# An encoder's feed-forward layers: the norm's factor goes through a VectorE copy ahead of the tokens' low parts and is transposed later; the memory's squares come in two halves

## The chip, the cores and the metric

One core of a Trainium2 chip runs the kernel. The metric is the device time of one execution in microseconds (us), the median of several runs. TensorE does the matrix products, VectorE and ScalarE prepare operands and read results, GpSimd does small things and issues DMAs that add into a tile, and SyncE issues the plain loads. Matrix operands lie in SBUF, products in eight PSUM banks (four tagged `pa`, four `pb`).

## The reference

Two encoder layers work on 512 tokens of width 1024 in float32. Each layer is a feed-forward layer, a mixer (attentions of several kinds), an attention to a memory of 256 rows, and a second feed-forward layer, each behind an RMS norm:

```python
def rmsnorm(x, g):
    xf = x.astype(jnp.float32)
    y = xf * lax.rsqrt(jnp.mean(xf * xf, axis=-1, keepdims=True) + EPS)
    return (y * g.astype(jnp.float32)).astype(x.dtype)

def swiglu(x, wg, wu, wd):
    return (jax.nn.silu(x @ wg) * (x @ wu)) @ wd
```

The hidden width of `swiglu` is 2816, which is 22 blocks of 128. The norm's factor of a token (the reciprocal root of the mean of its squares) scales whole rows of the products, so the kernel multiplies the gained but unscaled tokens and applies the factor to the products' results. The memory's rows are normed too, and only the attention to the memory uses them.

## The kernel before, in words

**Products.** A float32 product is made of three passes with rounded operands: high by high, token's low by weight's high, token's high by weight's low. ScalarE makes the high part of an operand (`wh`, `sh`, `t1h` and the like) by a rounding copy, VectorE the low part (`wl`, `sl`, `t1l`) as the rest. Every weight thus costs a load (SyncE), a 128x1024 copy on ScalarE and a 128x1024 subtraction on VectorE.

**A feed-forward layer** (`ffn`; there are four, called first to fourth FFN here). `plain_pair` computes blocks 0 and 1 of the hidden width directly: a gate product and an up product for each (line L316). Behind the second block's gate product TensorE transposes the tokens' summed squares (L249), VectorE sums them (L251, tile `s`) and makes the mean (L258, `v`), GpSimd raises it to the power -0.5 (L242, `r`), TensorE transposes `r` spread over 128 columns (L328, four of them), and VectorE copies the outcome to `R` (L329). `R` scales the gate products (L332, `gs`) and goes into the hidden values.

Blocks 2 to 21 are done as ten pairs by seven products of a quarter's size in place of eight (a Strassen-like scheme). `token_sums` makes the scheme's four combinations of tokens, t1 to t4 (L366), with their high (L370, ScalarE) and low parts (L373 and L375, VectorE). For each pair `open_pair` multiplies quarter w11 with tokens x11; `sum_pair` makes the sum of two quarters (`s`, loaded by SyncE and added into by a GpSimd DMA, L460), multiplies it with t1 (here: product T1), subtracts w11 from it (L464) and multiplies with t2 (product T2); `cross_pair` multiplies w12 with x21 (here: the x product), fetches `s3`, negates it on ScalarE (L482), adds to it by a GpSimd DMA (L483) and multiplies with t3 (T3); `close_pair` does the rest. Each of these is 24 matmuls of 128x256 (L430). `operand` (L408, L409) makes a weight's parts; its numbers in the first pair are used below: n0 is w11, n1 the sum, n2 the sum less w11, n3 w12, n4 `s3`, n5 the next pair's w11. Every third (n2, n5) has its own buffers `sh` and `sl`; the others take turns in two buffers `wh` and two `wl`.

**Order.** TensorE's order is the program's. The other engines' order is made by a scheduler that follows when results are due; `high_priority()` moves work ahead, and `behind(ins)` keeps what follows on an instruction's engine behind it.

**The memory's squares.** `mem_stats` runs once, in the first FFN after pair 2: eight blocks of 128x256 are loaded by SyncE (L1104), squared on ScalarE (L218, L221), summed on GpSimd (L222), then transposed and reduced as above. TensorE meets the two transposes of the sum between two products of pairs.

Of the kernel before, what the change touches and what calls it, by code (L numbers as in the profile page):

```python
# [11 lines left out]
F32 = mybir.dt.float32  # L12
# [7 lines left out]
P = 128  # L20
# [3 lines left out]
KB = D // P  # L24
FB = F // P
QB = S // P
NMEM = 256
# [38 lines left out]
LEAD, REST = ((0, 0), (0, 1)), ((1, 0),)  # L66

CHUNKS = (8, 8, 6)
LAMBDA_INIT = 0.8 - 0.6 * math.exp(0.0)

L0_CHUNKS = [[(2120, 256), (2632, 256)], [(3144, 512)], [(2376, 256), (2888, 256)],
# [33 lines left out]
class Encoder:  # L105
# [157 lines left out]
    def ffn(self, pre):  # L263


        with ExitStack() as ctx:
            pool = lambda name: ctx.enter_context(self.tc.tile_pool(name=pre + name, bufs=1))
            f = self.f = SimpleNamespace(pre=pre, hp=pool("h"), tp=pool("t"), H={}, n=0, last=None)
            self.plain_pair()
            ends = [sum(CHUNKS[:c + 1]) // 2 for c in range(len(CHUNKS))]  # L270
            c = 0
            pair = self.open_pair(1)
            for p in range(1, FB // 2):
                final = p == FB // 2 - 1
                self.sum_pair(pair)
                if p in ends:
                    self.down(c)
                    c += 1
                self.cross_pair(pair)
                if final:  # L280
                    early = self.block(c, 0, True)
                    self.down_products(c, early, LEAD + REST, False)
                    self.close_pair(pair, True)
                    self.down(c, early)
                else:
                    old, pair = pair, self.open_pair(p + 1)
                    self.close_pair(old, False)
                if p == 2 and self.mem_r is None:
                    self.mem_stats()

    def plain_pair(self):
        nc, I, f = self.nc, self.I, self.f
        xs, order = self.xs, self.order
        self.wshare = 0
        banks = []
        for b in range(2):
            ws, self.ws = self.ws, None
            after = self.rest if b == 0 and self.chained else None
            ws = ws or [self.wload(I[f.pre + w][b], 1024, after) for w in ("wg", "wu")]
            pp = [self.bank("pa"), self.bank("pb" if b else "pa")]  # L300
            banks.append(pp)
            if b == 0:
                head = order[:KB // 2]
                groups = [(ks, ((0, 0), (0, 1))) for ks in (head, order[KB // 2:KB - 1], order[KB - 1:])]
                if self.mem_r is None:
                    groups[1:1] = [(head, ((1, 0),))]
                    groups.append((order[KB // 2:], ((1, 0),)))
                else:
                    groups.append((order, ((1, 0),)))
            else:  # L310
                groups = [(order, ((0, 0), (0, 1), (1, 0)))]
            for ks, ops in groups:
                for w, p in zip(ws, pp):
                    for a, c in ops:
                        for k in ks:
                            nc.tensor.matmul(p, w[a][:, k * P:(k + 1) * P], xs[k][c],  # L316
                                             start=k == order[0] and a == c == 0, stop=k == order[-1] and a == 1)
                    if b == 1 and p is pp[0]:
                        with self.tc.high_priority():
                            v, r = self.stats(self.acc, QB)  # L320
        f.after, f.led = self.loaded, self.leading
        with self.behind(self.summed), self.behind(self.squared):
            self.token_sums()
        p = self.bank("pb")
        f.R = f.tp.tile([P, S], F32, name="R", tag="R", bufs=1)
        with self.tc.high_priority():
            for i in range(QB):
                nc.tensor.transpose(p[:, i * P:(i + 1) * P], r[:, i:i + 1].to_broadcast([P, P]), self.ident)  # L328
            nc.vector.tensor_copy(f.R, p)  # L329
        gs = f.tp.tile([P, 1024], F32, name="gs", tag="gs")  # L330
        for b in range(2):
            nc.vector.tensor_mul(gs[:, b * S:(b + 1) * S], banks[b][0], f.R)  # L332
        self.hidden(0, gs, [pp[1] for pp in banks])
# [12 lines left out]
    def hidden_parts(self, p, h, b0):  # L346
        nc, f = self.nc, self.f
        if p not in f.H:
            f.H[p] = [f.hp.tile([P, 1024], F32R, name=n, tag="H", bufs=CHUNKS[0]) for n in ("hh", "hl")]
        hh, hl = f.H[p]  # L350
# [5 lines left out]
    def token_sums(self):  # L356

        nc, f = self.nc, self.f
        xs, gain = self.xs, self.col(self.norm)
        half = KB // 2  # L360
        one, two = slice(0, 256), slice(256, 512)
        part = lambda t, k: t[:, (k % half) * 256:(k % half) * 256 + 256]
        g = lambda k: gain[:, k:k + 1]

        def combine(out, k, tokens, op, other):
            nc.vector.scalar_tensor_tensor(part(out, k), self.x[k][:, tokens], g(k), part(other, k), op0=OP.mult, op1=op)  # L366

        def parts(name, t, sign=1.0):
            h = f.tp.tile([P, 1024], F32R, name=name + "h", tag=name + "h")
            nc.scalar.activation(h, t, AF.Copy, scale=sign)  # L370
            l = f.tp.tile([P, 1024], F32R, name=name + "l", tag=name + "l")
            if sign == 1.0:
                nc.vector.tensor_sub(l, t, h.bitcast(F32))  # L373
            else:
                nc.vector.scalar_tensor_tensor(l, t, sign, h.bitcast(F32), op0=OP.mult, op1=OP.subtract)  # L375
            return [(part(h, k), part(l, k)) for k in range(half)]

        lead, rest = range(half), range(half, KB)
        room = [f.tp.tile([P, 2048], F32, name="tq", tag="gu", bufs=2) for _ in range(2)]
        x12, t1, t2, t3 = (t[:, o:o + 1024] for t in room for o in (0, 1024))  # L380
        for k in lead:
            nc.scalar.activation(part(x12, k), self.x[k][:, two], AF.Copy, scale=g(k))
        for k in lead:
            combine(t1, k, one, OP.subtract, x12)
        T1 = parts("t1", t1, -1.0)
        for k in rest:
            combine(t2, k, two, OP.add, t1)
        T2 = parts("t2", t2)
        for k in rest:
            combine(t3, k, two, OP.subtract, x12)  # L390
        T3 = parts("t3", t3)
        t4 = x12
        for k in rest:
            combine(t4, k, one, OP.subtract, t2)
        T4 = parts("t4", t4)
        quarters = lambda ks, tokens: [tuple(x[:, tokens] for x in xs[k]) for k in ks]
        f.B = {"11": quarters(lead, one), "21": quarters(rest, one), "22": quarters(rest, two),
               "1": T1, "2": T2, "3": T3, "4": T4}
# [141 lines left out]
    def block(self, c, d, own=False):  # L540

        nc, f = self.nc, self.f
        n = CHUNKS[c] * P
        src = self.I[f.pre + "wd"][d, :, sum(CHUNKS[:c]) * P:sum(CHUNKS[:c]) * P + n]
        if not own:
# [7 lines left out]
    def down_products(self, c, block, ops, tail):  # L553

        f = self.f
        (w, bank), nb = block, CHUNKS[c]
        for a, e in ops:
            for j in range(nb - 2, nb) if tail else range(nb - 2):
                b = sum(CHUNKS[:c]) + j
                h = f.H[b // 2][e][:, b % 2 * S:b % 2 * S + S]  # L560
# [532 lines left out]
            nc.vector.scalar_tensor_tensor(kl[:, sl], p, gcol, kh.bitcast(F32)[:, sl], op0=OP.mult, op1=OP.subtract)  # L1093
        return kh, kl, vp

    def mem_stats(self):
        nc = self.nc
        with ExitStack() as ctx:
            mp = ctx.enter_context(self.tc.tile_pool(name="ms", bufs=2))
            acc, loaded, leading, powed = None, self.loaded, self.leading, self.powed  # L1100
            for k in range(KB):
                m = mp.tile([P, NMEM], F32, name="mem", tag="mem", bufs=4)
                with self.behind(loaded):
                    nc.sync.dma_start(m, self.I["memT"][k * P:(k + 1) * P, :])  # L1104
                with self.behind(powed), self.behind(leading):
                    acc = self.square(acc, m, NMEM, mp)
            v, r = self.stats(acc, 2)
            self.mem_r = self.const.tile([P, 2], F32, name="mem_r")
            nc.vector.tensor_copy(self.mem_r, r[:, 0:2])
            self.mem_epsv = self.const.tile([P, 2], F32, name="mem_epsv")  # L1110
            nc.vector.tensor_scalar(self.mem_epsv, v[:, 0:2], EPS, None, op0=OP.mult)
# [417 lines left out]
```

## Time and profile before

| what | value |
|---|---|
| runs, us | 2157.35, 2159.32, 2159.65 |
| median, us | 2159.32 |
| the profiled execution's own time, us | 2162.13 |
| its span from first to last instruction, us | 2160.3 |
| TensorE busy | 2101.7 us, 97% of the span |
| VectorE, ScalarE, GpSimd busy | 73%, 53%, 17% |
| mean granted TensorE clock | 0.992 of full |

The span is what the profile shows, and 1.8 us lie around it. Busy shares are means over many stages. The chain that ended last tells which engine sets the time where; a wait of TensorE on that chain is time that something else costs. A timeline row gives start, duration, engine, line, operation and tiles, and in brackets the idle time before it with what ended it.

### The profile page before, as it was taken

What the parts mean: (1) busy time and instruction counts of PE and PEld (TensorE: products, weight loads), DVE (VectorE), ACT (ScalarE), POOL (GpSimd) and SP (SyncE); (2) the same over time, 40 slices, a digit from 0 to 9 for tenths busy, and PEclk for the clock granted to TensorE, in tenths of its full rate; (3) what the DMA queues carried; (4) which work ended last, traced back from release to release, by engine and by line L of the source; (5) the groups of instructions that cost most, each with busy time, mean ns of one, the idle gap of its engine ahead of it and who ended that gap; (6) DMA issues with size and microseconds to landing.
All of it is one profiled execution on the core that took longest, in us unless ns stands there. A gap on an engine that the chain in (4) does not pass through costs nothing.

```text
span 2160.3 us, 32514 instructions
## 1 busy us (share of the span) xinstructions
PE 2101.7 (97%) x12830; PEld 1877.6 (87%) x12834; DVE 1575.2 (73%) x2242; ACT 1137.2 (53%) x1701; POOL 376.2 (17%) x319
## 2 busy tenths in 40 slices
PE   7999999998999989999999999999999998999999
PEld 5989998787778879898989899988888877989997
DVE  7757668479876788585788677685668677857666
ACT  5535444465686565253455355344678555625442
POOL 1200002336332120000020000013443022000000
PEclk9999999999999999999999999999999999999999
DMA  6646633321232257365346466334223225646532
GB/s 204 181 123 180 163 99 125 141 74 65 70 130 73 79 151 187 111 187 146 91 143 183 139 167 173 103 110 161 79 87 128 88 69 146 165 123 180 162 102 91
DMA packets 86122, 279.65 MB, mean 129 GB/s; under 512 B 9681, under 2 KB 12881, under 8 KB 85969
## 3 DMA queue, kind: packets, MB, share of 16 engines
q1 hardware_dynamic: 74448, 235.62, 32.5%
q0 software_dynamic: 11520, 41.95, 11.0%
q8 instruction: 101, 1.65, 0.3%
q14 instruction: 53, 0.43, 0.1%
HBM read 271.24 MB, written 6.29 MB: 128 GB/s over the span
## 4 chain that ended last, share of the span: by engine, by line
PE 86%; DVE 8%; ACT 2%; issue 1%; POOL 1%; DMA 1%; SPq 0%; DVEq 0%; POOLq 0%; ACTq 0%
PE ps_pa L430 26%; PE ps_pb L430 11%; PE ps_pa L663 10%; PE ps_pa L561 10%; PE ps_pb L561 9%; PE ps_pa L614 4%; PE ps_pa L316 2%; PE ps_pb L769 2%; PE ps_pa L1203 1%; PE ps_pb L821 1%; PE ps_pa L1060 1%; PE ps_pb L794 1%; DVE wl L157 1%; DVE xl L205 1%; PE ps_pa L979 1%
## 5 line engine op out<-in xcount | busy, mean ns | idle before, releaser
L155 ACT ACTIVATE wh<-wf 128x1024 fp32r<-128x1024 f32 (+2 forms) x211 | 215.5, 1023 | 356.4 <-PE ps_pa L561 120.9
L157 DVE TENSOR_TENSOR wl<-wf,wh 128x1024 fp32r<-128x1024 f32 (+2 forms) x169 | 200.3, 1188 | 50.4 <-ACT wh L155 47.8
L409 DVE TENSOR_TENSOR wl<-s,wh 128x1024 fp32r<-128x1024 f32 x108 | 132.3, 1225 | 71.9 <-ACT wh L408 69.5
L408 ACT ACTIVATE wh<-s 128x1024 fp32r<-128x1024 f32 x108 | 114.3, 1059 | 103.8 <-PE ps_pb L430 40.5
L408 ACT ACTIVATE wh<-wf 128x1024 fp32r<-128x1024 f32 x84 | 89.1, 1061 | 132.0 <-PE ps_pa L430 45.8
L483 POOL DMA_DIRECT2D s<-l_ffn_wq x40 | 35.6, 889 | 532.0 <-ACT s L482 532.0
L157 POOL TENSOR_TENSOR wl<-wf,wh 128x1024 fp32r<-128x1024 f32 x42 | 101.8, 2425 | 141.6 <-ACT wh L155 140.0
L663 PE MATMUL ps_pa<-wh,xh 128*128 128x512 f32 x384 | 123.4, 403 | 0.0
L663 PE MATMUL ps_pa<-wh,xl 128*128 128x512 f32 x384 | 119.9, 393 | 0.0
L663 PE MATMUL ps_pa<-wl,xh 128*128 128x512 f32 x384 | 119.4, 392 | 0.0
L460 POOL DMA_DIRECT2D s<-l_ffn_wq x40 | 35.7, 891 | 463.7 <-DMA s<-l_ffn_wq 391.6
L409 DVE TENSOR_TENSOR wl<-wf,wh 128x1024 fp32r<-128x1024 f32 x84 | 102.8, 1224 | 12.9 <-ACT wh L408 12.8
L571 DVE TENSOR_TENSOR dn<-ps_pa,R 128x512 f32<-128x512 f32 x48 | 33.1, 690 | 88.6 <-PE ps_pa L561 88.3
L222 POOL TENSOR_TENSOR acc<-acc,sq 128x512 f32<-128x512 f32 (+1 forms) x37 | 52.2, 1411 | 251.9 <-ACT sq L221 250.8
L561 PE MATMUL ps_pb<-hh,wh 128*128 128x512 f32 x352 | 95.5, 389 | 0.0
L561 PE MATMUL ps_pb<-hl,wh 128*128 128x512 f32 x352 | 95.4, 389 | 0.0
L561 PE MATMUL ps_pb<-hh,wl 128*128 128x512 f32 x352 | 95.4, 389 | 0.0
L561 PE MATMUL ps_pa<-hh,wh 128*128 128x512 f32 x328 | 88.8, 390 | 0.0
L561 PE MATMUL ps_pa<-hh,wl 128*128 128x512 f32 x328 | 88.6, 389 | 0.0
L561 PE MATMUL ps_pa<-hl,wh 128*128 128x512 f32 x328 | 88.6, 389 | 0.0
L663 PEld LDWEIGHTS ps_pa<-wh,xl 128*128 128x128 f32 x384 | 72.7, 189 | 16.1
L663 PEld LDWEIGHTS ps_pa<-wl,xh 128*128 128x128 f32 x384 | 72.6, 189 | 16.0
(376 smaller groups left out, 5973.1 us busy)
## 6 DMA issues: line engine op xcount, KB each, us to landing
wf<-l_ffn_wq SPq DMA_DIRECT2D x120, 512.0 KB, 3.3
s<-l_ffn_wq SPq DMA_DIRECT2D x80, 512.0 KB, 4.5
s<-l_ffn_wq POOLq DMA_DIRECT2D x80, 512.0 KB, 6.6
wf<-l_ffn_wd SPq DMA_DIRECT2D x64, 512.0 KB, 4.0
wf<-l_w_in SPq DMA_DIRECT2D x48, 512.0 KB, 3.2
wf<-l_ffn_wd SPq DMA_DIRECT2D x32, 384.0 KB, 3.1
wf<-l_mem_wkv SPq DMA_DIRECT2D x16, 512.0 KB, 3.3
wf<-l_w_out SPq DMA_DIRECT2D x16, 512.0 KB, 3.2
```

Of the source, the lines that this page charges most:

```text
L155: self.leading = nc.scalar.activation(wh[:, sl], w[:, sl], AF.Copy)
L157: eng.tensor_sub(wl[:, sl], w[:, sl], wh.bitcast(F32)[:, sl])
L222: self.summed = (eng or nc.gpsimd).tensor_add(acc[:, :n], acc[:, :n], sq[:, :n])
L316: nc.tensor.matmul(p, w[a][:, k * P:(k + 1) * P], xs[k][c], start=k == order[0] and a == c == 0, stop=k == order[-1] and a == 1)
L408: self.leading = nc.scalar.activation(h, t, AF.Copy)
L409: nc.vector.tensor_sub(l, t, h.bitcast(F32))
L430: self.nc.tensor.matmul(bank[:, sl], w[a][:, o:o + P], xs[k][b], start=first and z == a == b == k == 0, stop=z == a == 1 and k == KB // 2 - 1,
L460: nc.gpsimd.dma_start(pair.s, self.quarter(p, 2), accum_op=OP.add)
L561: self.nc.tensor.matmul(bank, w[a][:, j * P:(j + 1) * P], h, start=j == a == e == 0, stop=j == nb - 1 and (a, e) == ops[-1])
L614: nc.tensor.matmul(banks[dd], a[:, o:o + P], parts(k)[b], start=k == first and a is wh and b == 0, stop=k == last and a is wl)
L663: nc.tensor.matmul(banks[i], xs[k][a][:, i * P:(i + 1) * P], w[b][:, kk * 512:kk * 512 + 512], start=k == a == b == 0, stop=k == KB - 1 an ...
L769: nc.tensor.matmul(bank[:, o:o + n], a, b[:, :n], start=c == 0, stop=c == len(ops) - 1)
```

## The change

It has three parts. First, `r` is copied by VectorE into a tile `factor` as soon as it is there, and everything that `parts` issues (the high and low parts of t1 to t4) is kept behind that copy on the copy's engine: VectorE. Second, the four transposes, the copy to `R` and the hidden values of the plain pair move into a function that is called after `open_pair(1)`, so that they stand behind the first pair's first product. Third, the memory's squares are issued in two halves of four blocks, after pairs 3 and 4, and their sum is transposed after pair 6; the condition that they stand behind a power on GpSimd is dropped.

```diff
-            self.plain_pair()
+            R = self.plain_pair()
...
             pair = self.open_pair(1)
+            R()
...
-                if p == 2 and self.mem_r is None:
-                    self.mem_stats()
+                if self.mem_r is None:
+                    self.mem_stats(p)
...
                         with self.tc.high_priority():
-                            v, r = self.stats(self.acc, QB)
+                            r = self.stats(self.acc, QB)[1]
+                            factor = self.small.tile([P, 4], F32, name="factor", tag="factor")
+                            f.factored = nc.vector.tensor_copy(factor, r)
         f.after, f.led = self.loaded, self.leading
         with self.behind(self.summed), self.behind(self.squared):
             self.token_sums()
+        return lambda: self.plain_end(banks, factor)
+
+    def plain_end(self, banks, r):
+        nc, f = self.nc, self.f
         p = self.bank("pb")
...
         def parts(name, t, sign=1.0):
+            with self.behind(f.factored):
+                return parts_of(name, t, sign)
...
+MEM_SQUARES, MEM_FACTOR = (3, 4), 6
...
+            for k in range(MEM_SQUARES.index(p) * n, MEM_SQUARES.index(p) * n + n):
...
-                with self.behind(powed), self.behind(leading):
-                    acc = self.square(acc, m, NMEM, mp)
-            v, r = self.stats(acc, 2)
+                with self.behind(leading):
+                    f.macc = self.square(f.macc, m, NMEM, f.mp)
+        if p == MEM_FACTOR:
+            v, r = self.stats(f.macc, 2)
```

What it moves on the engines follows in rows of the two programs' orders. Line numbers of the changed kernel are higher by 2 to 13.

VectorE in the first FFN, before, from the low part of t1 on. `wl<-s_396` is operand n1, `s_396<-s_396,wf` the subtraction of w11, `wl<-wf` operand n3.

```order
L375 SCALAR_TENSOR_TENSOR t1l<-tq,t1h 128x1024
L366 SCALAR_TENSOR_TENSOR tq<-x,cols,tq 128x256
L373 TENSOR_TENSOR t3l<-tq,t3h 128x1024
L258 TENSOR_SCALAR v<-s 128x4
L366 SCALAR_TENSOR_TENSOR tq<-x,cols,tq 128x256
L409 TENSOR_TENSOR wl<-s_396,wh 128x1024
L373 TENSOR_TENSOR t2l<-tq,t2h 128x1024
L373 TENSOR_TENSOR t4l<-tq,t4h 128x1024
L464 TENSOR_TENSOR s_396<-s_396,wf 128x1024
L329 COPY R<-ps_pb 128x512
L409 TENSOR_TENSOR wl<-wf,wh 128x1024
L332 TENSOR_TENSOR gs<-ps_pa,R 128x512 x2
```

The same place in the changed kernel:

```order
L260 TENSOR_SCALAR v<-s 128x4
L375 SCALAR_TENSOR_TENSOR tq<-x,cols,tq 128x256
L422 TENSOR_TENSOR wl<-s_398,wh 128x1024
L325 COPY factor<-r 128x4
L388 SCALAR_TENSOR_TENSOR t1l<-tq,t1h 128x1024
L386 TENSOR_TENSOR t2l<-tq,t2h 128x1024
L386 TENSOR_TENSOR t3l<-tq,t3h 128x1024
L386 TENSOR_TENSOR t4l<-tq,t4h 128x1024
L477 TENSOR_TENSOR s_398<-s_398,wf 128x1024
L338 COPY R<-ps_pb 128x512
L422 TENSOR_TENSOR wl<-wf,wh 128x1024
L422 TENSOR_TENSOR wl<-s_491,wh 128x1024
```

`v` is two large instructions earlier; the copy of the factor stands behind n1, and all four low parts behind the copy. Behind these rows `gs` and then the low part of n2 follow in the changed kernel, so n4 (`wl<-s_491`) now precedes both. In the second and fourth FFN `v` also moves ahead of t1l and t3l, n0 stands ahead of the copy, and n1 behind t4l.

VectorE in the third FFN, before:

```order
L375 SCALAR_TENSOR_TENSOR t1l<-tq,t1h 128x1024
L373 TENSOR_TENSOR t3l<-tq,t3h 128x1024
L373 TENSOR_TENSOR t2l<-tq,t2h 128x1024
L373 TENSOR_TENSOR t4l<-tq,t4h 128x1024
L409 TENSOR_TENSOR wl<-wf,wh 128x1024
L251 TENSOR_REDUCE s<-ps_pb 128x4
L258 TENSOR_SCALAR v<-s 128x4
L409 TENSOR_TENSOR wl<-s_11058,wh 128x1024
L329 COPY R<-ps_pb 128x512
L464 TENSOR_TENSOR s_11058<-s_11058,wf 128x1024
L332 TENSOR_TENSOR gs<-ps_pa,R 128x512 x2
L409 TENSOR_TENSOR wl<-wf,wh 128x1024
```

and in the changed kernel:

```order
L422 TENSOR_TENSOR wl<-wf,wh 128x1024
L253 TENSOR_REDUCE s<-ps_pb 128x4
L260 TENSOR_SCALAR v<-s 128x4
L325 COPY factor<-r 128x4
L388 SCALAR_TENSOR_TENSOR t1l<-tq,t1h 128x1024
L386 TENSOR_TENSOR t2l<-tq,t2h 128x1024
L386 TENSOR_TENSOR t3l<-tq,t3h 128x1024
L386 TENSOR_TENSOR t4l<-tq,t4h 128x1024
L422 TENSOR_TENSOR wl<-s_11064,wh 128x1024
L338 COPY R<-ps_pb 128x512
L422 TENSOR_TENSOR wl<-wf,wh 128x1024
L477 TENSOR_TENSOR s_11064<-s_11064,wf 128x1024
```

Here the four low parts, which stood ahead of everything, moved behind the power and its copy. `gs`, n4 and the low part of n2 follow.

ScalarE in the first FFN, before, around operands n2 (`sh<-s_396`) and n4 (`wh<-s_489`):

```order
L450 COPY gu<-ps_pa 128x2x256
L408 ACTIVATE sh<-s_396 128x1024
L408 ACTIVATE wh<-s_489 128x1024
L340 ACTIVATE t<-gs 128x1024
L408 ACTIVATE sh<-wf 128x1024
L467 COPY gu<-ps_pa 128x2x256
L482 ACTIVATE s_1009<-s_1009 128x1024
```

and in the changed kernel, where `s_955` is pair 3's `s3`:

```order
L463 COPY gu<-ps_pa 128x2x256
L421 ACTIVATE wh<-s_491 128x1024
L421 ACTIVATE sh<-s_398 128x1024
L349 ACTIVATE t<-gs 128x1024
L495 ACTIVATE s_955<-s_955 128x1024
L421 ACTIVATE sh<-wf 128x1024
L480 COPY gu<-ps_pa 128x2x256
```

n4 now stands ahead of n2, and the negation of `s3` ahead of n5 (`sh<-wf`) and of the copy of T2's outcome; so it is in all four FFNs.

## Rows read from the trace of the kernel before

**Rows 1.** The page: the chain that ended last, by engine.

```profile
PE 86%; DVE 8%; ACT 2%; issue 1%; POOL 1%; DMA 1%; SPq 0%; DVEq 0%; POOLq 0%; ACTq 0%
```

**Rows 2.** Waits of TensorE: total us, times, longest.

```profile
PE ps_pb L328 <- POOL r L242: 18.4, 3, 7.5
```

**Rows 3.** Timeline, first FFN, TensorE: start, us, engine, line, operation.

```profile
31.93 1.98 PE L316 MATMUL ps_pb<-xh,wl 128*128 128x512 f32 x8
...
46.49 0.64 PE L430 MATMUL ps_pb<-t1h,wh 128*128 128x256 f32 x4
...
49.37 0.64 PE L430 MATMUL ps_pa<-t2h,sh 128*128 128x256 f32 x4
...
52.98 0.64 PE L430 MATMUL ps_pa<-xh,wh 128*128 128x256 f32 x4
```

**Rows 4.** Timeline, first FFN, VectorE, with GpSimd's power.

```profile
35.59 5.75 POOL L242 TENSOR_TENSOR r<-v,mhalf 128x4 f32<-128x4 f32 x1 [4.81 <-DVE v L258]
...
38.08 1.22 DVE L373 TENSOR_TENSOR t4l<-tq,t4h 128x1024 fp32r<-128x1024 f32 x1
39.21 1.23 DVE L464 TENSOR_TENSOR s<-s,wf 128x1024 f32<-128x1024 f32 x1
...
48.50 1.28 DVE L332 TENSOR_TENSOR gs<-ps_pa,R 128x512 f32<-128x512 f32 x2
```

**Rows 5.** Timeline, first FFN, ScalarE.

```profile
49.09 1.06 ACT L408 ACTIVATE wh<-s 128x1024 fp32r<-128x1024 f32 x1 [0.33 <-PE ps_pb L430]
```

**Rows 6.** Timeline, second FFN: ScalarE, GpSimd, TensorE.

```profile
783.00 1.04 ACT L408 ACTIVATE wh<-wf 128x1024 fp32r<-128x1024 f32 x1
...
785.94 5.35 POOL L242 TENSOR_TENSOR r<-v,mhalf 128x4 f32<-128x4 f32 x1 [3.58 <-DVE v L258]
...
803.33 0.64 PE L430 MATMUL ps_pa<-xh,wh 128*128 128x256 f32 x4
```

**Rows 7.** Timeline, third FFN: ScalarE, GpSimd, TensorE.

```profile
1132.82 1.06 ACT L408 ACTIVATE wh<-wf 128x1024 fp32r<-128x1024 f32 x1 [0.38 <-DMA wf<-l_ffn_wq]
...
1137.90 1.04 POOL L242 TENSOR_TENSOR r<-v,mhalf 128x4 f32<-128x4 f32 x1 [6.21 <-DVE v L258]
...
1143.25 0.64 PE L430 MATMUL ps_pb<-t1h,wh 128*128 128x256 f32 x4
...
1149.01 0.64 PE L430 MATMUL ps_pa<-xh,wh 128*128 128x256 f32 x4
```

**Rows 8.** Timeline, fourth FFN: GpSimd, TensorE.

```profile
1825.21 5.35 POOL L242 TENSOR_TENSOR r<-v,mhalf 128x4 f32<-128x4 f32 x1 [4.19 <-DVE v L258]
...
1841.90 0.64 PE L430 MATMUL ps_pa<-xh,wh 128*128 128x256 f32 x4
```

**Rows 9.** Timeline, the memory's squares: ScalarE, then TensorE.

```profile
86.68 0.75 ACT L221 ACTIVATE sq<-mem 128x256 f32<-128x256 f32 x2 [3.29 <-DMA mem<-memT]
...
91.30 0.69 PE L249 MATMUL ps_pb<-ident,acc 128*128 128x128 f32 x2 [3.60 <-POOL acc L222]
91.64 1.20 PE L430 MATMUL ps_pb<-t1h,wh 128*128 128x256 f32 x4
...
96.74 0.64 PE L430 MATMUL ps_pa<-t2h,wh 128*128 128x256 f32 x4
```

**Rows 10.** Windows: stretch, us, busy (count) of PE, PEld, DVE, ACT, POOL, clock, DMA, GB/s.

```profile
91.00:95.00 4.00, 3.70 (x18) 3.70 (x19) 3.99 (x5) 0.00 (x0) 0.24 (x1) 0.50 0.92 157
571.00:575.00 4.00, 4.00 (x15) 3.37 (x14) 3.38 (x7) 3.04 (x5) 0.00 (x0) 0.58 0.00 0
```

**Rows 11.** Timeline, TensorE, in the first mixer.

```profile
569.14 0.63 PE L794 MATMUL ps_pb<-ident,e 128*128 128x128 f32 x2 [2.90 <-DVE e L921]
```

**Rows 12.** Timeline, first FFN, SyncE's queue, then ScalarE.

```profile
52.08 0.33 SPq L417 DMA_DIRECT2D s<-l_ffn_wq  x1
...
55.40 1.06 ACT L482 ACTIVATE s<-s 128x1024 f32<-128x1024 f32 x1 [1.17 <-DMA s<-l_ffn_wq]
```

**Rows 13.** The page: DMA issues, KB each, median us to landing.

```profile
s<-l_ffn_wq SPq DMA_DIRECT2D x80, 512.0 KB, 4.5
```

More of the change, by code (lines that the diff above doesn't have):

```diff
@@ L267, in ffn @@
             pool = lambda name: ctx.enter_context(self.tc.tile_pool(name=pre + name, bufs=1))
-            f = self.f = SimpleNamespace(pre=pre, hp=pool("h"), tp=pool("t"), H={}, n=0, last=None)
-            self.plain_pair()
+            f = self.f = SimpleNamespace(pre=pre, ctx=ctx, hp=pool("h"), tp=pool("t"), H={}, n=0, last=None)
+            R = self.plain_pair()
             ends = [sum(CHUNKS[:c + 1]) // 2 for c in range(len(CHUNKS))]
@@ L368, in parts, with parts_of @@
         def parts(name, t, sign=1.0):
+            with self.behind(f.factored):
+                return parts_of(name, t, sign)
+        def parts_of(name, t, sign):
             h = f.tp.tile([P, 1024], F32R, name=name + "h", tag=name + "h")
@@ L1094, in mem_keys, with mem_stats @@
         return kh, kl, vp
[L1096 to L1102, printed above, removed]
+    def mem_stats(self, p):
+        nc, f = self.nc, self.f
+        if p in MEM_SQUARES:
+            if p == MEM_SQUARES[0]:
+                f.mp = f.ctx.enter_context(self.tc.tile_pool(name="ms", bufs=2))
+                f.macc = None
+            loaded, leading = self.loaded, self.leading
+            n = KB // len(MEM_SQUARES)
+            for k in range(MEM_SQUARES.index(p) * n, MEM_SQUARES.index(p) * n + n):
+                m = f.mp.tile([P, NMEM], F32, name="mem", tag="mem", bufs=4)
                 with self.behind(loaded):
                     nc.sync.dma_start(m, self.I["memT"][k * P:(k + 1) * P, :])
-                with self.behind(powed), self.behind(leading):
-                    acc = self.square(acc, m, NMEM, mp)
-            v, r = self.stats(acc, 2)
+                with self.behind(leading):
+                    f.macc = self.square(f.macc, m, NMEM, f.mp)
+        if p == MEM_FACTOR:
+            v, r = self.stats(f.macc, 2)
             self.mem_r = self.const.tile([P, 2], F32, name="mem_r")
```

## The prediction

> **What bounds the kernel now.** I read the chain that ended last first: TensorE holds 86% of it, VectorE 8%, GpSimd 1% [rows 1]. So only what TensorE waits for, or does more slowly, can move the time. Of TensorE's waits the largest is that of the four transposes for the norm's factor: 18.4 us in three waits, 7.5 the longest [rows 2]. The reader is to see that three of the four FFNs have it. In the first FFN the up product ends at 33.91 (31.93+1.98), the first pair's T1 starts at 46.49, T2 at 49.37 and the x product at 52.98 [rows 3]. A T product undisturbed takes 2.88 (49.37-46.49), a sixth of it 0.48.
>
> Why the power is late stands in [rows 4]: it starts at 35.59 and lasts 5.75, while VectorE runs one 128x1024 instruction after another, every 1.13 (39.21-38.08), the last ending at 40.44. The power ends 0.90 behind that. In the second and fourth FFN it takes 5.35 [rows 6, 8], in the third, where VectorE has no work, 1.04 [rows 7]. I read this as: beside back-to-back VectorE work the power gets through only when VectorE pauses.
>
> The Trainium skill (SBUF — State Buffer, section "SBUF: two separate sides") says that VectorE and GpSimd share a port pair as an exclusive lock, and that whichever instruction starts first has it for its whole length. The rows agree that the two exclude each other, but not that the power gets its turn at the end of the running instruction. From 35.59 to 40.44 it sat through some four of them. By the rule alone it would get in sooner, which is a rival below.
>
> The other wait is the memory's: 3.60 ahead of the two transposes, and behind it T1 took 5.10 (91.64 to 96.74) where 2.88 is usual [rows 9], at a granted clock of 0.50 [rows 10], which is the lower level, 1.2 GHz.
>
> **The FFNs, worked out.** I follow VectorE to the x product's start, after which TensorE was fully fed before. Durations: 1.13 for each 128x1024 on VectorE in a row, 1.22 for the last one to its end; 1.19 for the two `gs` [rows 4]; 0.65 for the copy of `R`, half of that pair; 1.06 for a rounding on ScalarE [rows 5]. The factor's copy is in no row; it lies between nothing and 1.13, and with 4 columns in place of 1024 I take 0.1.
>
> First FFN. `v` loses t1l and t3l ahead of it, so the power starts 2.26 sooner, at 33.33. n1's low part needs a buffer that the up product frees at 33.91; it runs to 35.17. VectorE then has only the factor's copy, so the power ends 0.90 later, 36.07. Low parts start at 36.2: four of them and the subtraction end at 41.94, n2's rounding at 43.0. T2 would be due at 39.97 (33.91, two products of 2.88 and 0.3 for four transposes, from 0.69 for two at the lower clock [rows 9]). So a new wait of 3.1 opens there. Behind the subtraction come R, n3, n4, `gs`, and n2's low part, which ends at 47.17. T2's third sixth needs it, having come there at 44.0: another 3.1. The x product starts 4x0.48 later, 49.1, against 52.98: gain **3.9**.
>
> Second FFN. The power starts at 783.68. n0's rounding ends at 784.04 [rows 6], its low part at 785.30, the power at 786.2. Four low parts follow from 786.35, n1's low part runs 790.87 to 792.1, and T1's third sixth waits for it; T2 is due at 794.05. Then R, n3, the subtraction to 795.0, the rounding to 796.1: T2 waits 2.0. `gs`, n4, n2's low part end at 798.46, T2's third sixth waits 1.4; x starts at 800.4, against 803.33: gain **2.9**. The fourth is the same, 1039.27 later by the two powers' starts: 1839.7 against 1841.90, gain **2.2** [rows 6, 8].
>
> Third FFN. Before, all low parts were done ahead of the power and nothing waited. Now n0's rounding ends at 1133.88 [rows 7], its low part at 1135.1, the sum and `v` at 1135.9, the power at 1137.0. Low parts to 1141.6, n1's to 1142.85, in time for T1 at 1143.25 as before. But R, n3 and the subtraction take VectorE to 1146.45, and n2's rounding, behind n4's on ScalarE, ends at 1147.9: T2, due at 1146.13, waits 1.8. `gs`, n4 and n2's low part end at 1149.95 (1.1 more); x starts at 1151.9 against 1149.01: **loss 2.9**.
>
> Sum: 3.9+2.9+2.2-2.9 = 6.1 gained, if TensorE's clock stays up.
>
> **What the new waits cost in clock.** A wait of 2.90 [rows 11] was followed by a stretch at 0.58, one of 3.60 by T1 at 0.50, which cost 2.22 [rows 9, 10]. The new waits are between 1.1 and 3.1. Each FFN's pair of them may cost nothing or 2.2. I take 1.5 in the first, which is nearest to the rows, 1.0 in the second and fourth, 0.5 in the third: **4.0**.
>
> **ScalarE's new order.** The negation of pair 3's `s3` now stands ahead of n5's rounding and the copy of T2's outcome, without which T3 can't start. Its load is issued when n4's low part ends; it landed 3.3 after its issue (52.08 to 55.40) [rows 12]. In the second FFN that gives 797.3+3.3+1.06+0.97+0.5 = 803.2 (the copy taken as half a rounding, having half the columns), and T3 is due at 800.4+2.88 = 803.3: 0.1 to spare, likewise in the third and fourth. In the first 1.3 are left. The median landing is 4.5 [rows 13], which would cost 1.1 in each of three. Bounds: nothing to 3.3; I take the middle, **1.5**, since the rows of this place lie at the lower end and the page's median above it.
>
> **The memory.** Before, squares waited 3.29 for the second load group [rows 9]. Now each half fits the four buffers, so its loads wait for no square of its own half, the halves stand a pair apart, and the transposes come some three pairs later. A pair is seven products of 2.88, 20 us, so the sum is long done. Gain: 3.60+2.22 = **5.8**. The number of GpSimd's additions and ScalarE's squares stays; each half lies beside TensorE's products, in a stage where GpSimd is nearly free. Were that cover gone, one half's additions would delay a pair's accumulating DMA (rival below).
>
> **Sum.** 6.1-4.0-1.5+5.8 = 6.4 us gained. The profiled execution took 2162.13 and would take 2155.7; it lies 2.8 above the median of the runs, 2159.32, from which I forecast **2152.9**. A measurement of this kernel can tell about 0.2%, 4.3 us, from no change.
>
> **Rivals.**
> (a) The clock stays full through waits of 1 to 3 us. For it: no row shows a fall behind a wait below 2.9. Then 4.0 come back: 2148.9. Chance 0.12.
> (b) The power gets in at the end of the VectorE instruction that runs when it is issued. In the first FFN it would run ahead of n1's low part, which saves 0.3 to 0.4; in the second and fourth 0.3 each: 1.0 more gain, 2151.9. Against it: the three long powers. Chance 0.06. This is what the Trainium skill's lock (SBUF — State Buffer, "SBUF: two separate sides") would make of it; the rows agree only as far as that the two block each other.
> (c) The clock falls by the full 2.2 in all four FFNs, 8.8 in place of 4.0: 2157.7, no change that counts. For it: the waits come in pairs, 3 to 6 us in sum. Chance 0.12.
> (d) The memory's sum, or the accumulating DMA behind the additions, still holds up a product: the 5.8 are not gained, 2158.7. For it: loads of memory stand in SyncE's queue between weights. Chance 0.08.
> (e) The change does not do what it says: the power's length isn't VectorE's doing and stays 5.35 to 5.75. Then everything in the first FFN is 3.0 later than worked out, in the second and fourth 2.8, and the FFNs lose 2.5 instead of gaining 6.1: 2161.5, no change. Against it: the third FFN's 1.04. Chance 0.06.
> (f) Slower: the negation's load. Each us of landing over 3.4 (4.6 in the first FFN) delays T3 in each FFN, because n5 and the copy queue behind. At 7.0 the loss is 3x3.6+2.4 = 13.2 in place of 1.5: 2164.6. It decides from 6.8 on. For it: the median of this load is already 4.5 [rows 13]. Against it: 3.3 at this place [rows 12]. Chance 0.10.
>
> **The numbers.** The forecast has 0.46. Faster: forecast, (a), (b), 0.64. Within 0.2% (2155.0 to 2163.6): (c), (d), (e), 0.26. Slower: 0.10. The range 2148.0 to 2159.0 holds all but (e), (f) and a little of the forecast's own spread.
>
> **What would show it.** Right: powers of about 1.0 to 2.7 us in all FFNs; the wait for the factor gone from TensorE's list; new waits of T1 and T2 for `sh`, `wl`, `sl` of 1 to 3 us, those of the third FFN among them; x products at about 49.1 in the first FFN; no wait at the memory's transposes, now behind pair 6. Wrong: powers still above 5; granted clock of 1.0 or of 0.5 throughout the first pair; ScalarE idle at the negation, with TensorE waiting at T3; a product of pairs 4 to 6 waiting for an accumulated sum.

## The result, and the profile after

| | before | changed |
|---|---|---|
| median, us | 2159.08 | 2141.99 |
| runs, us | 2157.35 to 2159.65 | 2138.36 to 2143.13 |
| the profiled execution's time, us | 2162.13 | 2142.44 |
| its span, us | 2160.3 | 2140.7 |

The ratio of changed to before is 0.9919, with a 95% interval of 0.9902 to 0.9936: 17.5 us less by this ratio, where 6.4 were forecast and the range began at 2148.0. The direction was right, the size was not. One execution of e2 and one of e4 below took 2535 and 2957 us at mean granted clocks of 0.765 and 0.654; medians and ratios leave them out.

The page of the changed kernel, its first and its chain section (busy us, share, instructions by engine; then the chain by engine):

```profile
PE 2089.6 (98%) x12834; PEld 1859.6 (87%) x12834; DVE 1573.6 (74%) x2246; ACT 1137.5 (53%) x1701; POOL 366.1 (17%) x319
...
PE 86%; DVE 9%; ACT 2%; issue 1%; DMA 1%; POOL 0%; SPq 0%; DVEq 0%; POOLq 0%; ACTq 0%
```

GpSimd is gone from the chain [rows 1]. But TensorE's busy time itself fell, from 2101.7 to 2089.6, although it has the same work: 12.1 us that no wait explains. That is the number to follow.

The waits of TensorE in the changed kernel (total us, times, longest):

```profile
PE ps_pa L443 <- ACT sh L421: 8.3, 4, 3.1
...
PE ps_pa L443 <- DVE sl L422: 6.0, 4, 2.8
PE ps_pb L443 <- DVE wl L422: 3.2, 2, 1.8
```

The 18.4 us for the factor [rows 2] and the memory's 3.6 are gone; in their place stand 17.5 us: for operand n2 (`sh`, `sl`) in all four FFNs, for n1 (`wl`) in two. These are the new waits of the forecast.

The timeline of the first FFN, changed kernel: GpSimd, VectorE, TensorE, ScalarE.

```profile
33.88 1.21 POOL L244 TENSOR_TENSOR r<-v,mhalf 128x4 f32<-128x4 f32 x1 [2.40 <-DVE v L260]
...
33.70 0.48 DVE L375 SCALAR_TENSOR_TENSOR tq<-x,cols,tq 128x256 f32<-128x256 f32 x1
34.15 1.23 DVE L422 TENSOR_TENSOR wl<-s,wh 128x1024 fp32r<-128x1024 f32 x1
35.29 0.17 DVE L325 COPY factor<-r 128x4 f32<-128x4 f32 x1
...
30.71 1.98 PE L319 MATMUL ps_pb<-xh,wl 128*128 128x512 f32 x8
...
42.26 0.74 PE L443 MATMUL ps_pa<-t2h,sh 128*128 128x256 f32 x4 [3.09 <-ACT sh L421]
...
46.37 1.23 PE L443 MATMUL ps_pa<-t2h,sl 128*128 128x256 f32 x4 [2.84 <-DVE sl L422]
...
49.95 0.71 PE L443 MATMUL ps_pa<-xh,wh 128*128 128x256 f32 x4
...
33.07 1.04 ACT L421 ACTIVATE wh<-s 128x1024 fp32r<-128x1024 f32 x1
...
50.30 0.57 ACT L480 COPY gu<-ps_pa 128x512 f32<-128x512 f32 x1
```

The power takes 1.21 where it took 5.75 [rows 4], and T2 waits 3.09 and 2.84. From the up product's last pass to the x product it is 19.24 us (30.71 to 49.95); before it was 21.05 [rows 3]. Behind the second wait the last four sixths of T2 took 3.58 us in place of 1.92. The windows view shows the granted clock around it, 0.57, not far above the lower of its two levels, 1.2 GHz (stretch, us, busy and count of PE, PEld, DVE, ACT, POOL, granted clock, DMA share, GB/s):

```profile
43.00:51.00 8.00, 5.16 (x30) 4.90 (x29) 7.43 (x9) 3.77 (x5) 0.92 (x1) 0.57 0.44 147
```

The same distance in the other FFNs, changed against before: 17.46 against 19.41, 13.81 against 10.88, 17.37 against 18.70. The gains are 1.8, 1.9, -2.9 and 1.3, in sum 2.2 us. In the first two FFNs the slow stretch reaches into the x product: T3 starts 2.94 and 3.28 behind its start, where 2.88 is usual, so that counted up to T3 the gain is 1.7. The third FFN, which had no wait, now has two:

```profile
1131.70 0.74 PE L443 MATMUL ps_pa<-t2h,sh 128*128 128x256 f32 x4 [1.62 <-ACT sh L421]
1133.77 0.74 PE L443 MATMUL ps_pa<-t2h,sl 128*128 128x256 f32 x4 [0.85 <-DVE sl L422]
```

The memory's squares, changed kernel, GpSimd's two groups of additions and TensorE's transposes:

```profile
97.32 3.85 POOL L224 TENSOR_TENSOR acc<-acc,sq 128x256 f32<-128x256 f32 x3 [1.43 <-ACT sq L223]
161.34 5.59 POOL L224 TENSOR_TENSOR acc<-acc,sq 128x256 f32<-128x256 f32 x4 [0.24 <-ACT sq L223]
...
207.31 0.38 PE L251 MATMUL ps_pb<-ident,acc 128*128 128x128 f32 x2
```

The sum is there 40 us before it is wanted, and the transposes wait for nothing [rows 9].

So 2.2 us from the FFNs and some 6 from the memory are seen. The rest is in the matmuls themselves. Grouped by line and tiles (count, then busy us and mean ns of one, the pipelined time included), before:

```profile
L561 PE MATMUL ps_pb<-hh,wh 128*128 128x512 f32 x352 | 95.5, 389 | 0.0
...
L430 PE MATMUL ps_pa<-xl,sh 128*128 128x256 f32 x192 | 30.9, 283 | 0.0
L430 PE MATMUL ps_pa<-t2l,wh 128*128 128x256 f32 x192 | 30.9, 283 | 0.0
...
L430 PE MATMUL ps_pa<-t3l,sh 128*128 128x256 f32 x96 | 15.4, 283 | 0.0
```

and changed:

```profile
L574 PE MATMUL ps_pb<-hh,wh 128*128 128x512 f32 x352 | 96.3, 392 | 0.0
...
L443 PE MATMUL ps_pa<-xl,sh 128*128 128x256 f32 x192 | 30.0, 278 | 0.0
...
L443 PE MATMUL ps_pa<-t2l,wh 128*128 128x256 f32 x192 | 29.6, 276 | 0.0
...
L443 PE MATMUL ps_pa<-t3l,sh 128*128 128x256 f32 x96 | 15.4, 282 | 0.0
```

Every 128x256 product of t with `wh`, and of x with `sh`, is 3 to 10 ns shorter; t with `sh` is not, and the 128x512 products of the hidden values are 3 ns longer. From start to start (worked out from the trace's starts within groups of equal tiles), before's matmuls stand 120 ns apart almost without exception; the changed kernel's t with `wh` stand mostly 113, 114, 117 or 118 ns apart. The built program shows what differs: the tile `factor` has two buffers of 32 bytes among the small tiles, and everything allocated behind them (`hh`, `hl`, t1 to t4, `sh`, `sl`, `gu`) lies 64 bytes higher in each partition. Taken modulo 256 bytes, x, `xh`, `wh`, `wl` and t1 to t4, `sh`, `hh` all lay at 0; now x and `wh` lie at 0, t, `sh` and `hh` at 64.

**Theory P**: a 128x256 matmul goes faster where its two operands lie at different offsets, so the new tile, not the new order, brought some 10 us. **Rival S**: the order did it.

### The profile page after: what moved, and what is told of

Its sections match the earlier page's. It is cut to its first block, busy times and chain, and to the rows that moved or that the text cites. A ratio compares the mean times of both kernels' runs of the same rounds, so it can differ in the third digit from the quotient of the medians.

```text
span 2140.7 us, 32519 instructions
## 1 busy us (share of the span) xinstructions
PE 2089.6 (98%) x12834; PEld 1859.6 (87%) x12834; DVE 1573.6 (74%) x2246; ACT 1137.5 (53%) x1701; POOL 366.1 (17%) x319
## 4 chain that ended last, share of the span: by engine, by line
PE 86%; DVE 9%; ACT 2%; issue 1%; DMA 1%; POOL 0%; SPq 0%; DVEq 0%; POOLq 0%; ACTq 0%
PE ps_pa L443 26%; PE ps_pa L676 11%; PE ps_pb L443 10%; PE ps_pa L574 10%; PE ps_pb L574 10%; PE ps_pa L627 4%; PE ps_pa L319 2%; PE ps_pb L782 2%; PE ps_pb L834 1%; DVE xl L207 1%; PE ps_pa L1073 1%; PE ps_pb L807 1%; DVE wl L159 1%; PE ps_pa L1221 1%; PE ps_pa L992 1%
## 5 line engine op out<-in xcount | busy, mean ns | idle before, releaser
L584 DVE TENSOR_TENSOR dn<-ps_pb,R 128x512 f32<-128x512 f32 x48 | 33.0, 688 | 73.5 <-PE ps_pb L574 73.1
```

The source lines that it names most:

```text
L584: nc.vector.tensor_mul(t, bank, f.R)
```

## The experiments

**e1, addresses alone.** The kernel before, with 64 bytes more padding; order and instructions equal.

```diff
-PAD_SMALL = 80
+PAD_SMALL = 96
```

> The kernel before with a padding tile that is 64 bytes longer, so that every tile allocated behind the small tiles (t1 to t4, sh, sl, hh, hl) lies 64 bytes higher, as it does in the changed kernel; no instruction and no order differs from before. Theory P (the new factor tile moved the operands, and TensorE's 128x256 matmuls go at 113 to 118 ns instead of 120 wherever the two operands' addresses differ by the shift): about 10 us faster than before, 2147 to 2151. Rival S (the gain beyond the forecast comes from the order of the work): 2159, no change, matmuls at 120 ns.

Measured: ratio 0.9962 (0.9950 to 0.9975), 8.2 us faster without one instruction moved. The page of e1, busy time by engine:

```profile
PE 2093.8 (97%) x12830; PEld 1863.3 (87%) x12834; DVE 1572.2 (73%) x2242; ACT 1136.3 (53%) x1701; POOL 375.1 (17%) x319
```

and two of its groups:

```profile
L430 PE MATMUL ps_pa<-xl,sh 128*128 128x256 f32 x192 | 30.0, 278 | 0.0
L430 PE MATMUL ps_pa<-t2l,wh 128*128 128x256 f32 x192 | 29.6, 276 | 0.0
```

TensorE's busy time fell by 7.9, and the groups have the changed kernel's means to the nanosecond. P stands.

**e2, the change without the new addresses.** The changed kernel, 64 bytes less padding.

```diff
-PAD_SMALL = 80
+PAD_SMALL = 64
```

> The changed kernel with the padding 64 bytes shorter, so that the large tiles lie at the addresses of before; no instruction and no order differs from the changed kernel. Theory P: the matmuls are back at 120 ns and the time at 2150 to 2153, 6 to 9 us below before. Rival S: 2142, as the changed kernel.

Measured: 0.9976 (0.9965 to 0.9986), 5.2 us faster than before, median 2153.86. The page of e2:

```profile
PE 2101.3 (98%) x12830; PEld 1877.1 (87%) x12834; DVE 1578.3 (73%) x2246; ACT 1137.3 (53%) x1701; POOL 366.9 (17%) x319
```

and one of its groups:

```profile
L443 PE MATMUL ps_pa<-t2l,wh 128*128 128x256 f32 x192 | 30.9, 283 | 0.0
```

TensorE's busy time is back. This is the change that was forecast, at the addresses that the forecast took for granted.

**e3, the memory's halves alone**, and **e4, the factor alone** (the copy, the low parts behind it, the later transposes), both at before's addresses. e3 leaves `plain_pair` and `parts` as before; e4 keeps the old `mem_stats` and has `PAD_SMALL = 64`.

> The kernel before with only the memory's squares in two halves; addresses as before. Both theories: the wait of 3.6 us and the slow T1 behind it are gone, 2153 to 2154, 5.8 us faster. If the squares still hold up a product, less than 2 us.

Measured: 0.9980 (0.9970 to 0.9989), 4.3 us; the memory's wait is gone from TensorE's list.

> The kernel before with only the factor's copy, the low parts behind it and the later transposes; addresses as before. Theory P: the first, second and fourth FFN gain 1.4 to 1.8 us each and the third loses about 3.2, 2157 to 2158. Rival S (the order brings all of the rest): 2147 to 2149.

Measured: 0.9993 (0.9981 to 1.0005), 1.5 us, with no change at all inside the interval; median 2156.35, near what P has and far from S. The parts add up within their noise: 8.2, 4.3 and 1.5 are 14.0, against 17.5 for all, each good to 2 to 4 us either way. The addresses are worth 8.2 by e1 against before and 12.3 by the changed kernel against e2; the intervals meet. An estimate from the traces' starts lies between: the change in the mean distance of undisturbed matmuls of each kind, times their number, gives 10.9 us for e1 and 11.3 for the changed kernel against e2. T with `wh` goes from 120.0 to 116.0 ns and x with `sh` from 120.0 to 115.3; the hidden products lose, from 226.9 to 229.1.

**e5, the third FFN as before.** Its low parts are not kept behind the copy.

```diff
-            with self.behind(f.factored):
+            with self.behind(None if f.pre == "l1_ffn1_" else f.factored):
```

> The changed kernel, but in the third FFN alone the low parts of t1 to t4 are not kept behind the factor's copy, so that they stand ahead of the power as before; addresses as in the changed kernel. Theory A (where VectorE had no queue in front of the power, the copy ahead of the low parts only adds waits): the third FFN's waits for sh, sl go and the x product starts about 3 us earlier, 2139. Theory B (the low parts' place is worth something in all four): 2142 or more.

Measured: 0.9908 (0.9893 to 0.9923), median 2138.50. The third FFN's distance falls from 13.81 to 11.54 (1119.37 to 1130.91), and of its two waits 0.48 is left. The trace shows this; by the times alone, e5 and the changed kernel are not told apart.

**e6, no rule on the low parts in any FFN.** The copy and the later transposes stay.

```diff
-            with self.behind(f.factored):
-                return parts_of(name, t, sign)
+            return parts_of(name, t, sign)
```

> The changed kernel without the rule that the low parts stand behind the factor's copy, in all four FFNs; the copy, the late transposes and the memory's halves stay, and so do the addresses. The power is then issued behind two more large VectorE instructions in three FFNs and should last beside VectorE again, some 4 to 5 us. Theory A (the FFNs gain by the later transposes alone): the transposes wait 2 to 4 us for the factor, but T2 no longer waits for sh and sl: 2130 to 2138. Theory B (the early power is what brings the FFNs' gain): 2144 to 2148.

Measured: 0.9883 (0.9866 to 0.9901), median 2135.33, 6.7 below the changed kernel. In e6, from TensorE's waits:

```profile
PE ps_pb L337 <- DVE factor L325: 8.7, 3, 4.1
```

and from the timeline of the first FFN:

```profile
34.89 4.61 POOL L244 TENSOR_TENSOR r<-v,mhalf 128x4 f32<-128x4 f32 x1 [4.68 <-DVE v L260]
...
39.77 0.91 PE L337 MATMUL ps_pb<-ident,factor 128*128 128x128 f32 x4 [4.07 <-DVE factor L325]
...
30.85 1.98 PE L319 MATMUL ps_pb<-xh,wl 128*128 128x512 f32 x8
...
44.63 0.64 PE L442 MATMUL ps_pa<-t2h,sh 128*128 128x256 f32 x4
...
47.50 0.63 PE L442 MATMUL ps_pa<-xh,wh 128*128 128x256 f32 x4
```

The power lasts 4.61 again and the transposes wait 4.07 for it. Yet T2 waits for nothing there, and the x product comes at 47.50, with the up product's last pass at 30.85: 16.65 us against 19.24. In the other FFNs it is 15.37, 11.55 and 15.37, against 17.46, 13.81 and 17.37. The early power was bought with four VectorE instructions ahead of n2, and that was the dearer place. Theory A stands, as far as the copy stays (e12).

**e12, e6 without the copy.** The transposes read `r` itself; the padding keeps the addresses.

```diff
-                            factor = self.small.tile([P, 4], F32, name="factor", tag="factor")
-                            f.factored = nc.vector.tensor_copy(factor, r)
...
-        return lambda: self.plain_end(banks, factor)
+        return lambda: self.plain_end(banks, r)
```

> As e6, but without the factor's copy: the later transposes read the power's result directly; the padding is 64 bytes longer, so that the large tiles keep the addresses of the changed kernel. VectorE then has no instruction that waits for the power, and runs on to the subtraction of w11 and the copy of R. Theory C (the copy's worth is that it makes VectorE pause, which lets the power through): the power lasts about 1.1 us longer in three FFNs, 2137 to 2140. Rival (the copy does nothing): 2135 as e6.

Measured: 0.9933 (0.9909 to 0.9956), median 2144.11, 8.8 above e6 and more than expected, with executions from 2138.91 to 2150.30. The second FFN of e12, GpSimd and VectorE:

```profile
779.66 6.48 POOL L244 TENSOR_TENSOR r<-v,mhalf 128x4 f32<-128x4 f32 x1 [4.90 <-DVE v L260]
...
782.89 1.22 DVE L383 TENSOR_TENSOR t4l<-tq,t4h 128x1024 fp32r<-128x1024 f32 x1
784.02 1.22 DVE L474 TENSOR_TENSOR s<-s,wf 128x1024 f32<-128x1024 f32 x1
787.35 0.69 DVE L336 COPY R<-ps_pb 128x512 f32<-128x512 f32 x1 [2.11 <-PE ps_pb L335]
```

VectorE runs one instruction more, and the power is longer by just that: 6.48 against 5.35 in e6, ending 0.90 behind the subtraction (785.24, 786.14), as in [rows 4]. In the first FFN it is 5.75 against 4.61, in the fourth 6.49 against 5.35. So the pause that the copy forces ends the power 1.13 us sooner in three FFNs. The Trainium skill (SBUF — State Buffer, section "SBUF: two separate sides") gives the shared ports to whichever engine starts first, for its whole instruction; by that alone the power's turn would come behind the instruction that was running, and here it sat through five. The rest of e12's loss was not foreseen: the scheduler also put n2's low part behind `gs` and n4 in the first FFN, whose distance grew from 16.65 to 20.84. How much of the 8.8 is the pause and how much the other order, this run does not separate.

**e8, an offset of 32 bytes in place of 64**, and **e7, three offsets**: the hidden tiles at 0, t at 64, `sh` at 128.

```diff
-PAD_SMALL = 80
+PAD_SMALL = 72
```

> The changed kernel with 32 bytes less padding, so that the large tiles lie 32 bytes above the addresses of before and not 64. If any difference of offsets counts, 2142 as the changed kernel; if only 64 does, 120 ns everywhere and 2150 to 2154.

Measured: 0.9983 (0.9974 to 0.9993), 3.7 us faster than before, less than the first expectation and for a reason that neither had. The 128x512 products of hidden values became slower; TensorE's busy time and one group of e8:

```profile
PE 2103.8 (98%) x12834; PEld 1865.5 (87%) x12834; DVE 1574.7 (73%) x2246; ACT 1138.0 (53%) x1701; POOL 363.5 (17%) x319
...
L574 PE MATMUL ps_pb<-hh,wh 128*128 128x512 f32 x352 | 97.6, 395 | 0.0
```

From start to start they stand 234 ns apart in place of 227, which takes back all that the 128x256 products gain (t with `wh` mostly at 116 to 120): TensorE's busy time is 2103.8, where e2, the same order at an offset of 0, has 2101.3. So no gain by the addresses is seen, and the 3.7 us are no more than the order's 5.2 in e2. The offsets that help one shape can hurt another.

e7 is the changed kernel with `PAD_SMALL = 64` and tiles lengthened by some words:

```diff
-room = [f.tp.tile([P, 2048], F32, name="tq", tag="gu", bufs=2) for _ in range(2)]
+room = [f.tp.tile([P, 2048 + 8], F32, name="tq", tag="gu", bufs=2) for _ in range(2)]
...
-        f.R = f.tp.tile([P, S], F32, name="R", tag="R", bufs=1)
+        f.R = f.tp.tile([P, S + 16], F32, name="R", tag="R", bufs=1)[:, :S]
```

> The changed kernel with the same instructions in the same order, but other addresses: the hidden tiles (hh, hl) at offset 0 as before the change, t1 to t4 at 64, sh and sl at 128, x and wh, wl at 0 (bytes, modulo 256). Theory P (operands of a matmul at different offsets go faster): t with sh goes from 120 to 113 to 118 ns, hh with wh back from 229 to 227, and the time falls to 2133 to 2138. If an offset of 128 counts as none, x with sh goes back to 120 ns and the time is 2138 to 2142. Rival: the pitch depends on single addresses, not on pairs, and t with sh stays at 120.

Measured: 0.9913 (0.9897 to 0.9929), median 2141.36: no better than the changed kernel. The pairs did what P says: t with `sh` (64 apart) fell to mostly 113 and 114 ns and the hidden products to 227. But x with `sh` (128 apart) went back to 119 on average, spread from 115 to 122, and t with `wh`, whose own offsets were not touched, from a mix of 113 and 118 to mostly 118. What chooses between those two I did not find.

**e9, e6 with all 128x256 pairs 64 apart**, and **e10, the changed order at the same addresses**: as e7, and the sum of squares `acc` lengthened by 16 words, which moves `wh` and `wl`.

> As the kernel without the rule on the low parts (e6), with other addresses: x at offset 0, wh, wl, hh, hl at 64, t1 to t4 at 128, sh, sl at 192 (bytes, modulo 256), so that the operands of every 128x256 product differ by 64 and those of the 128x512 products of the hidden values agree. Theory P: x with wh and wl (some 2000 matmuls) falls from 120 to 113 to 118 ns, t with sh (some 1200) as well, hh with wh from 229 to 227; against it, 128x512 products of x with weights may lose 2 ns each. 2118 to 2128, where e6 took 2135. Rival: the pitch depends on something else that moved with the factor tile, and 2135 or more.

Measured: 0.9874 (0.9859 to 0.9888), median 2131.31, 4.0 below e6 where 7 to 17 were expected; the intervals of the two overlap. Groups of e9:

```profile
L573 PE MATMUL ps_pb<-hh,wh 128*128 128x512 f32 x352 | 95.4, 389 | 0.0
L442 PE MATMUL ps_pa<-xl,wh 128*128 128x256 f32 x448 | 69.8, 278 | 0.0
...
L442 PE MATMUL ps_pa<-t2l,wh 128*128 128x256 f32 x192 | 30.4, 279 | 0.0
...
L319 PE MATMUL ps_pa<-xh,wl 128*128 128x512 f32 x96 | 23.9, 396 | 0.0
```

The weights moved to 64 while x stayed at 0, and x with `wh` is now faster too, more than half of it at 113 or 114 ns: it is the pair that counts, not the t tiles. But the other three pairs, 64 apart as well, stand mostly at 117 to 119. And the 128x512 products of x with weights, now 64 apart, go from 228 to 233 ns from start to start (389 to 396 in the last group shown). By the estimate from the starts, e9 gains 5.4 us on e6, and would gain 3.7 more without that loss.

> The changed kernel with its order as it is and the addresses of e9. If order and addresses are separate causes, 6 to 8 us slower than e9, that is 2125 to 2135. If the addresses also change what the order costs, another difference.

Measured: 0.9903 (0.9888 to 0.9918), median 2137.97, 6.7 above e9. By the medians the order's price is 6.7 at both sets of addresses (7.8 and 6.3 by the ratios, each uncertain by some 5): nothing here shows that one cause changes the other.

**e11, only t4's low part behind the copy**, not in the third FFN, at e9's addresses:

```diff
-            with self.behind(f.factored):
+            with self.behind(f.factored if name in ("t4",) and f.pre != "l1_ffn1_" else None):
```

> As e9, but t4's low part alone stands behind the factor's copy, and not in the third FFN. VectorE then pauses for the power one large instruction sooner in the second and fourth FFN, while the subtraction of w11 stays where it is. Theory A (only the time of the pause counts for the transposes, and the subtraction for T2): up to 1 us faster than e9 in each of two FFNs, 0 to 2 us in all. Rival: no difference.

Measured: 0.9863 (0.9846 to 0.9879), median 2129.38, the fastest here, 1.4% below before. The powers of the second and fourth FFN lasted 4.21, one instruction less than e9's 5.35. Against e9 the intervals overlap, and the distances of these two FFNs differ by 0.2 and 0.1 only: not told apart.

## Why the prediction was wrong

**The step that failed** is a term that the sum put at nothing without a reason: a change in the pace of TensorE's matmuls. The sum took the durations of before's products ("A T product undisturbed takes 2.88") for those of after, and priced the factor's copy as an instruction alone: "it lies between nothing and 1.13, and with 4 columns in place of 1024 I take 0.1". As an instruction it took 0.17. But it needs a tile, the tile moves everything behind it by 64 bytes, and the matmuls changed their pace: 8.2 us in e1, 12.3 from e2 to the changed kernel, 12.1 us of busy time between the two traces. No rival held this either.

**The rest of the sum held, in part by luck.** e2 is the forecast's own case: forecast 6.4 us, measured 5.2, with an interval of 3.0 to 7.6. Its terms were off by some 1 to 2 us each, and their errors went opposite ways.
- *The power.* Forecast about 1.0 to 2.7 in all FFNs; it was 1.21, 1.04, 1.04 and 1.94.
- *The FFNs.* Forecast 2.1 in sum with the clock's charge; 2.2 in the changed kernel, 3.9 at the old addresses (17.87, 17.03, 13.80 and 17.45 in e2). Counted up to T3 it is 1.7 and 2.5. One by one: 2.4, 1.9, -3.4, 1.2 forecast; 1.8, 1.9, -2.9, 1.3 seen. The waits came where they were put: 3.1 and 3.1 in the first FFN (3.09, 2.84), 1.8 and 1.1 in the third (1.62, 0.85).
- *The clock.* 4.0 charged; the last four sixths of T2 took 1.7, 1.2, 0.1 and 1.5 us more than 1.92, in sum 4.5, and the x products of the first two FFNs 0.5 more. In e2 it was 4.4 and 1.4. Rivals (a) and (c) fell.
- *ScalarE's new order.* 1.5 charged, nothing lost: no wait at T3 is in the list. In the first FFN the copy of T2's outcome was at 50.30, T3 at 52.90. Rival (f) fell.
- *The memory.* 5.8 forecast, 4.3 measured in e3 (2.4 to 6.5); rival (d) fell.
- *Rivals (b) and (e).* The power did get shorter, so (e) fell. As for (b), what let the power in was a gap on VectorE and not the end of an instruction. In the fourth FFN there was no gap, and the power ended 0.90 behind n0's low part, as forecast. In the second VectorE stood idle for n0's rounding, and the power was over before n0's low part began. In the first, n1's low part waited for its rounding (33.07 to 34.11) and started 0.45 behind the instruction ahead of it, where 0.40 is the spacing without a gap. In this gap of 0.05 the power got through, ending at 35.09 beside n1's low part; 0.90 behind that part it would have been 36.28. So an early power came in two FFNs, by gaps that the forecast had not worked out, and the FFNs' gains show nothing of the rival's 1.0.

**What the forecast did not ask** is whether an early factor is worth its price. It worked out the new waits rightly and still called the sum a gain of the FFNs; e6 shows that the later transposes with the copy, but without the rule on the low parts, would have gained some 7 us more. Without the copy too, e12, the gain is no larger than the change's.

## What to carry to other kernels

A new tile, however small, can move every tile behind it: compare the operands' offsets before and after, and look at the mean time of one matmul by tiles before explaining a gain by order. A run with the padding changed and nothing else prices it. And before an engine is made to deliver early, count what is pushed behind: here a wait of 4 us for the factor was cheaper than four instructions ahead of the operand that was wanted next.

## What the runs showed of the hardware that was not expected

- TensorE's 128x256 float32r matmuls stood 120 ns apart where both operands lay at the same offset modulo 256 bytes, and mostly 113 to 119 where they lay 64 apart; 128 apart gave 119 on average (e7), 32 apart 117 to 118 (e8). The 128x512 products went the other way: those of hidden values 227 ns at equal offsets, 229 at 64, 234 at 32, those of x 228 at equal offsets and 233 at 64 (e9). That the addresses do it is shown; by what mechanism is open.
- A small GpSimd power beside back-to-back VectorE work on SBUF ended 0.90 us behind VectorE's last instruction in every case where VectorE left no gap: 5.75, 5.35, 4.61, 6.48, 4.21 and 1.94 us, according to how many instructions stood there, and 1.04 where VectorE had none. A gap of 0.05 us was enough to let it through (1.21, first FFN of the changed kernel).
